# The product with w_out by Strassen's method, one product after the other for half the rows

## The chip, the cores and the metric

The kernel runs on one core of a Trainium2 chip. The core has five engines that run side by side and wait for each other through semaphores: TensorE (matrix products into PSUM), VectorE, ScalarE, GpSimd, and SyncE, which here only issues DMAs. DMAs are issued from three queues: SyncE's (SP), GpSimd's (POOL) and ScalarE's. The metric is the time of one execution on the device, in microseconds (us). Three runs of the kernel before gave 1147.69, 1149.69 and 1149.91 us; their median is 1149.69.

## The reference

One layer over 1024 rows of 1024 channels, all in float32. The input is normalized and modulated, multiplied by w_in (1024 x 8192), and goes through two branches: a dilated attention and a gated linear recurrence of eight heads (HGRN2). Their outputs are multiplied by w_branch_a and w_branch_b, weighted and added to y (1024 x 1024). The end is what matters here:

```python
y = sigmoid(g_a) * (o_a @ w_branch_a) + sigmoid(g_b) * (o_b @ w_branch_b)
x = x + gate[:, None] * (y @ w_out)        # gate: one factor for each of 1024 columns, from c and w_ada
return x * rsqrt(mean(x * x, -1) + EPS) * final_g
```

## The kernel before, in words

**Numbers as two parts.** A float32 operand of a large product is split into a high part (rounded to fp32r by a ScalarE copy) and a low part (the difference, by VectorE). A product is then three matmuls: high by high, low by high, high by low (`mm3`, lines 238 to 241). `split` (line 243) makes both parts of a 128 x 512 piece in the ring tiles w_hi and w_lo, four deep.

**Products with w_in.** They already use Strassen's method in Winograd's form: `add_pair` (line 265) takes two columns of 128 of w_in, four pieces of 256 KB, and makes seven products of 12 matmuls in place of eight. Its preparation steps (`prep_s1`, `prep_12` and so on) are the sums and splits of the pieces. The right-hand blocks, made once from the normalized input, are called b11, b12, b21, b22, t1 to t4.

**The stream.** `Stream` (line 71) keeps all these steps in one list. `step` runs a quarter of a product; `ahead` emits the preparation of the two steps that follow (`AHEAD`, line 67). Pieces are loaded by SP into a ring of eight raw tiles; a load goes out when its tile's last use has been emitted. `put_off` keeps a pair's seventh product back until two products of the next unit have been queued.

**Stages.** After a start of some 100 us, attention runs (to about 455 us), with stream steps filled in between its own matmuls. Then the attention branch (`branch_a`, line 1001) to about 541, with the pairs of heads 0 and 1 ahead of it. Then the recurrence, eight heads of some 51 us (`recurrence`, line 1072): in seven levels VectorE multiplies kk and qb by decays (lines 1117 and 1119), TensorE multiplies the results in small products (lines 1085, 1104, 1113), and pairs of w_in for the later heads are filled in (`fill`). From about 965 on comes the recurrence's branch (`branch_b`, line 1225): eight units of 128 rows of y, m0 to m7, whose results are split into parts as they come (lines 1237 to 1241). Meanwhile `gate_sum` (line 1316) computes the gate from w_ada's last third, loaded by SP, and `add_wo` (line 1283) loads w_out by SP, multiplies it by the gate and splits it.

**The last stage** (lines 1391 to 1413) multiplies y by the gated w_out. For rows 0 to 511 the eight PSUM banks hold four row tiles of 1024 columns, and the inner index k runs outermost; the tiles of rows 512 to 1023 follow one after the other. That is eight products of half the rows, half the columns and half of k. `finish` adds the residual x, squares, takes the root (GpSimd, `pow`), scales by final_g and stores each row tile; the last tile is cut in pieces of 512, 256 and 256 columns.

**Order.** TensorE's order is the program's throughout. That of the other engines is chosen by a scheduler when the kernel is built; each then runs its own list in that order.

## Time and profile before

| what | value |
|---|---|
| median of three runs | 1149.69 us |
| the profiled execution's own time | 1151.74 us |
| its span, first to last instruction | 1149.9 us |
| TensorE busy | 1113.1 us, 97% |
| VectorE busy | 809.0 us, 70% |
| ScalarE busy | 517.8 us, 45% |
| moved by DMA | 189.54 MB, mean 165 GB/s |
| mean granted TensorE clock | 0.995 |

The profile names engines PE (TensorE matmul), PEld (its weight loads), DVE (VectorE), ACT (ScalarE), POOL (GpSimd) and SP (SyncE). A row of a group or of a timeline gives line, engine, operation and the tiles written and read (`out<-in`); a bracket tells how long the engine was idle before it and what released it. Times are microseconds from the start of the span. The matmul of 512 columns is recorded with 0.39 us, but a new one starts every 0.23 us: matmuls overlap.

### The profile page before, as it was taken

Reading aid. Unit: us, or ns where it says so; the run is one execution under the profiler, and the core shown is the slowest. Engines: PE = TensorE matmul, PEld = TensorE weight load, DVE = VectorE, ACT = ScalarE, POOL = GpSimd, SP = SyncE. Lnnn points to the kernel's source line nnn. Section 1 sums busy time; section 2 is a strip of 40 time slices with the busy share of each in tenths; the row PEclk is TensorE's granted clock in tenths of the full one; section 3 lists DMA queues with packets and bytes.
Section 4 is the critical chain, followed back from the end, with each engine's and each line's share of the span. In section 5 each row is a group of like instructions: output and inputs, shape, how many; then the busy total and the mean of one; then the engine's idle time right before and its main releaser. Section 6 shows DMA issues by size and latency. Waiting matters only on the chain.

```text
span 1149.9 us, 21616 instructions
## 1 busy us (share of the span) xinstructions
PE 1113.1 (97%) x8266; PEld 908.7 (79%) x8266; DVE 809.0 (70%) x1607; ACT 517.8 (45%) x1059; POOL 117.7 (10%) x195
## 2 busy tenths in 40 slices
PE   5899999999999999999999999999999999999997
PEld 2677788888888888788877878787887878888886
DVE  3458888888877776753687787878888773769053
ACT  4565555578555555542234434343443432334021
POOL 1103032122202201100000000000000011000000
PEclk9999999999999999999999999999999999999999
DMA  9718576565556533746635253444435289864052
GB/s 311 225 37 248 175 209 179 152 165 145 139 139 154 153 100 104 269 158 215 223 103 171 78 185 100 160 140 137 158 101 176 81 259 325 290 213 133 29 183 75
DMA packets 161480, 189.54 MB, mean 165 GB/s; under 512 B 11312, under 2 KB 107696, under 8 KB 161376
## 3 DMA queue, kind: packets, MB, share of 16 engines
q1 hardware_dynamic: 140080, 153.95, 41.9%
q0 software_dynamic: 20896, 33.60, 11.7%
q8 instruction: 65, 1.06, 0.4%
q10 hardware_dynamic: 400, 0.61, 0.2%
q14 instruction: 39, 0.32, 0.1%
HBM read 129.36 MB, written 58.76 MB: 164 GB/s over the span
## 4 chain that ended last, share of the span: by engine, by line
PE 82%; DVE 7%; issue 6%; DMA 2%; ACT 2%; POOL 1%; ACTq 0%; POOLq 0%; DVEq 0%; SPq 0%
PE m L239 16%; PE m L241 15%; PE m L240 15%; PE pq L240 5%; PE pq L239 5%; PE pq L241 5%; PE pp L1085 3%; PE po L927 2%; PE pt L912 2%; PE pss L895 1%; PE pss L894 1%; PE pou L1168 1%; PE pou L1170 1%; PE pou L1153 1%; PE pmod L572 1%
## 5 line engine op out<-in xcount | busy, mean ns | idle before, releaser
L224 DVE TENSOR_TENSOR w_lo<-w_raw,w_hi 128x512 fp32r<-128x512 f32 x156 | 106.7, 686 | 49.6 <-ACT w_hi L246 45.8
L246 ACT CAST w_hi<-w_raw 128x512 fp32r<-128x512 f32 x146 | 90.4, 620 | 56.6 <-PE m L241 46.6
L327 ACT COPY ct<-m 128x512 f32<-128x512 f32 x90 | 52.6, 585 | 89.9 <-PE m L241 72.7
L246 ACT CAST w_hi<-w_s 128x512 fp32r<-128x512 f32 x90 | 55.8, 620 | 75.7 <-PE m L241 50.3
L274 DVE TENSOR_TENSOR ct<-m,ct 128x512 f32<-128x512 f32 x90 | 61.8, 687 | 27.7 <-PE m L241 26.1
L224 DVE TENSOR_TENSOR w_lo<-w_s,w_hi 128x512 fp32r<-128x512 f32 x90 | 61.9, 688 | 11.7 <-ACT w_hi L246 10.0
L900 ACT ACTIVATE s<-s,st 128x128 f32<-128x128 f32 (+3 forms) x64 | 49.8, 778 | 32.1 <-DVE st L897 32.1
L916 ACT CAST pth<-pt 128x512 fp32r<-128x512 f32 (+1 forms) x80 | 43.6, 544 | 36.3 <-PE pt L912 31.9
L224 DVE TENSOR_TENSOR ptl<-pt,pth 128x512 fp32r<-128x512 f32 (+1 forms) x80 | 50.5, 632 | 7.7 <-ACT pth L916 7.0
L239 PE MATMUL m<-b11h,w_hi 128*128 128x512 f32 x124 | 52.5, 424 | 2.0 <-DVE ct L274 2.0
L1176 POOL TENSOR_TENSOR ssh<-ssh,halfh 128x4 f32<-128x4 f32 x16 | 18.0, 1127 | 345.8 <-DVE ssh L1175 345.8
L239 PE MATMUL m<-b21h,w_hi 128*128 128x512 f32 x124 | 51.3, 414 | 0.6 <-ACT w_hi L246 0.6
L239 PE MATMUL m<-b22h,w_hi 128*128 128x512 f32 x124 | 50.9, 411 | 0.1
L239 PE MATMUL m<-t1h,w_hi 128*128 128x512 f32 x120 | 50.5, 421 | 0.0
L239 PE MATMUL m<-t2h,w_hi 128*128 128x512 f32 x120 | 49.6, 413 | 0.8 <-ACT ct L327 0.8
L239 PE MATMUL m<-t4h,w_hi 128*128 128x512 f32 x120 | 49.7, 414 | 0.4 <-DVE ct L274 0.4
L239 PE MATMUL m<-t3h,w_hi 128*128 128x512 f32 x120 | 49.7, 414 | 0.0
L241 PE MATMUL m<-b11l,w_hi 128*128 128x512 f32 x124 | 49.6, 400 | 0.0
L240 PE MATMUL m<-b11h,w_lo 128*128 128x512 f32 x124 | 49.2, 397 | 0.0
L240 PE MATMUL m<-b21h,w_lo 128*128 128x512 f32 x124 | 48.6, 392 | 0.2 <-DVE w_lo L224 0.2
L241 PE MATMUL m<-b21l,w_hi 128*128 128x512 f32 x124 | 48.8, 393 | 0.0
L241 PE MATMUL m<-b22l,w_hi 128*128 128x512 f32 x124 | 48.7, 393 | 0.0
(358 smaller groups left out, 3191.2 us busy)
## 6 DMA issues: line engine op xcount, KB each, us to landing
w_raw<-in_w_in_dram SPq DMA_DIRECT2D x128, 256.0 KB, 3.4
wa<-in_w_ada_dram SPq DMA_DIRECT2D x16, 512.0 KB, 8.7
qk_d<-ct SPq DMA_DIRECT2D x32, 256.0 KB, 3.4
k<-qk_d POOLq DMA_DIRECT2D x64, 128.0 KB, 4.9
qp<-qk_d POOLq DMA_DIRECT2D x32, 128.0 KB, 4.4
toep<-toep_d POOLq DMA_DIRECT2D x8, 512.0 KB, 6.2
vq_d<-ct SPq DMA_DIRECT2D x16, 256.0 KB, 2.6
vq<-vq_d POOLq DMA_DIRECT2D x16, 256.0 KB, 4.1
```

Source lines behind the costliest of these rows:

```text
L224: nc.vector.tensor_tensor(out_, a, hi.bitcast(F32), ALU.subtract)
L239: nc.tensor.matmul(ps, ah, bh, start=start, stop=False, skip_group_check=more)
L240: nc.tensor.matmul(ps, al, bh, start=False, stop=False, skip_group_check=more)
L241: nc.tensor.matmul(ps, ah, bl, start=False, stop=stop, skip_group_check=more)
L246: nc.scalar.copy(hi, src)
L274: nc.vector.tensor_tensor(out_, a, b_, op)
L327: nc.scalar.copy(c[name], b[which])
L900: nc.scalar.activation(s[:, :kw], s[:, :kw], AF.Exp, bias=prev, scale=-1.0, accum_out=st2[:, 2:3])
L912: nc.tensor.transpose(pt[:, c0:c0 + P], pn[b][:, kt * P:(kt + 1) * P], ident)
L916: nc.scalar.copy(pth[:, :w], pt[:, :w])
L927: nc.tensor.matmul(po[:, 256 - n:256], vq[kt // 4][:, kt % 4], src[:, c0:c0 + n], start=kt == 0 and a == 0, stop=kt == 2 * j + 1 and a == 1)
L1085: nc.tensor.matmul(pl[32 * b:32 * b + 32, c], kk[:, o:o + 32], qb[:, 2 - n:2, o:o + 32], start=True, stop=True)
```

## The change

**Strassen's method for y @ w_out.** w_out's seven right-hand blocks (512 x 512 each: b11, b21, b22 and four combinations t1 to t4) are no longer gated. They are loaded, combined and split ahead of time, in 16 groups (`wo_group`: kind 0 to 3, k 0 to 3), and stored as high and low part in DRAM (`wo_d`, 14 blocks of 1 MB; two combinations also unsplit in `wt_d`). A group loads two pieces through the stream's ring. Each of the first pairs takes one group (`more`), whose one or two parts are emitted after `prep_12` and `prep_s3`; the units of `branch_a` share four groups (`post`). So three groups go with the pairs of heads 0 and 1, four with `branch_a`, and nine with the first nine pairs of the recurrence.

**branch_b.** y stays unsplit (four blocks `Y[kh, th]`). VectorE's order is the program's from here to the end. The gate is summed from four loads of 1 MB on POOL's queue instead of eight of 512 KB on SP's.

**The last stage** runs seven products one after the other, each over four row tiles of one half of the rows: 48 matmuls each. The left-hand blocks are made from y on the way (`y_s1` to `y_s4`, `y_12`, `y_22`). The right-hand blocks are loaded by POOL (`load_wo`), two products ahead, into two pairs of buffers. Results are first summed with what was kept, then multiplied by the gate, then added to x. Rows end (root, scaling, store) in steps that `end_on` emits one result later. In the attention branch, the first `branch_a` unit also changes: with `amid` the put-off product of the pair before runs in the middle of it.

```diff
@@ add_pair @@
+        others = more()
+        def other():
+            if others:
+                others.pop(0)()
...
         def prep_12():
             parts = split(T(i12))
             stream.done(i12)
+            other()
...
@@ add_unit(..., post=None, amid=False) @@
+        if amid:
+            owed, stream.owed = stream.owed, None
...
-                return parts
+                if kh == n - 1 and post:
+                    post()
+                return parts, owed and owed[0]()
...
                     if th == 0:
                         yield
+                        if owed:
+                            yield from owed[1](put_off)
+                            yield
...
+    WO = ("b11", "b21", "t1", "t2", "b22", "t3", "t4")
+
+    def wo_group(kind, k):
+        def load(src):
+            def go(n):
+                raw = raw_tile(n)
+                nc.sync.dma_start(raw.rearrange("p a b -> p (a b)"), src)
+                return raw
+            return stream.piece(go)
+        rows = lambda kh, c: w_out[(4 * kh + k) * P:(4 * kh + k + 1) * P, 512 * c:512 * c + 512]
+        ids = [load(src) for src in ((rows(0, 0), rows(0, 1)), (rows(0, 1), rows(1, 1)),
+                                     (wt_d[0, k], rows(0, 0)), (wt_d[1, k], rows(1, 0)))[kind]]
...
+        def keep(name, n):
+            for p, part in enumerate(split(T(n))):
+                nc.sync.dma_start(wo_d[2 * WO.index(name) + p][:, k], flat(part).bitcast(F32))
+        def combine(name, a, b_, op, n=None):
+            nc.vector.tensor_tensor(T(0), T(a), T(b_), op)
+            if n is not None:
+                nc.sync.dma_start(wt_d[n, k], flat(T(0)))
+            keep(name, 0)
+            stream.done(*ids)
+        return [[lambda: keep("b11", 0), lambda: combine("t1", 1, 0, ALU.subtract)],
+                [lambda: keep("b22", 1), lambda: combine("t3", 1, 0, ALU.subtract, 0)],
+                [lambda: combine("t2", 0, 1, ALU.add, 1)],
+                [lambda: keep("b21", 1), lambda: combine("t4", 1, 0, ALU.subtract)]][kind]
...
     with ExitStack() as mg:
+        mg.enter_context(tc.manual_schedule(engines={mybir.EngineType.DVE}))
...
+                nc.vector.tensor_tensor(Y[m // 4, th][:, m % 4], ya[th], gb[th], ALU.add)
...
-                    nc.vector.tensor_tensor(raw, raw, gate[:, half_of(c)], ALU.mult)
...
+        def load_wo(i):
+            pool, name = ((hpool, "t4"), (m1, "mb"))[i % 2]
+            wos[i] = [block(pool, name + p, F32R) for p in "hl"]
+            for p in range(2):
+                nc.gpsimd.dma_start(wos[i][p].bitcast(F32), wo_d[2 * i + p])
+        def split_y(src, slot):
+            ...
+            for k in (0, 2):
+                nc.scalar.copy(hi[:, k:k + 2], src[:, k:k + 2])
+                sub(lo[:, k:k + 2], src[:, k:k + 2], hi[:, k:k + 2])
...
+            def result(name, t0, c):
+                def f(n, ps):
+                    u, sl = kept[name][:, n], slice(512 * c, 512 * c + 512)
+                    if t0 + n == 7:
+                        xr, s4 = row(7)
+                        r = gated(ps[:, 256:], slice(256, 512))
+                        nc.vector.tensor_tensor(xr[:, 256:512], r, xr[:, 256:512], ALU.add)
+                    nc.vector.tensor_tensor(u, ps, u, ALU.add)
+                    nc.vector.tensor_tensor(u, u, gate[:, sl], ALU.mult)
+                    add_in(t0 + n, sl, u, c)
+                    end_on()
+                    if t0 == 0 and c == 1:
+                        end(t0 + n)
+                return f
+            def last(n, ps):
+                sl = slice(0, 512)
+                add_in(4 + n, sl, gated(ps, sl), 0)
+                end_on()
+                end(4 + n)
+            def last_part(a, ps):
+                ...
+                if a == 0:
+                    nc.vector.tensor_tensor(xo[:, 512:], xr[:, 512:], fg[:, 512:], ALU.mult)
+                add_in(7, sl, gated(ps, sl), 2 * a)
+                nc.vector.tensor_tensor(xo[:, sl], xr[:, sl], fg[:, sl], ALU.mult)
+                if a == 0:
+                    end_on()
+                    ...
+                    end_on()
...
+            prep = {0: [(1, y_12, None), (2, y_s1, (hpool, "b11"))], 2: [(3, y_s2, (hpool, "t1")), (4, y_s4, (m1, "ma"))],
+                    3: [(5, y_s3, (hpool, "b11")), (6, y_22, None)]}
+            plan = [(A, True, keep("p1")), ("B", True, result("p1", 0, 0)), ("C", True, keep("p5")),
+                    (A, False, keep("u2")), ("C", False, result("u2", 0, 1)), (A, False, result("p5", 4, 1)),
+                    (A, False, last)]
+            load_rows(range(4))
+            for i, (banks_, start, then) in enumerate(plan):
+                for j, y, slot in prep.get(i, ()):
+                    ys[j] = y(slot)
+                if i == 4:
+                    load_rows(range(4, 8))
+                ...
+                if i + 2 < 7:
+                    load_wo(i + 2)
```

`gated` multiplies a PSUM result by the gate; `add_in` adds it to the residual row and squares it on ScalarE; `end(t)` queues the two ending steps of a row tile (root on VectorE and GpSimd; scaling and store), of which `end_on` emits one per call for every tile under way. `combine` and `y_s1` to `y_s4` add or subtract blocks of y in two VectorE operations of 1024 columns each; `y_12` and `y_22` only split.

315 lines of the change are left out of this document (187 added, 128 removed).

## The prediction

> **What bounds the kernel now.** I read the page first (busy time, the chain that ended last), then the busy time by stage, then the instructions of the stage that changes and of the stages that receive its preparation.
>
> ```profile
> span 1149.9 us, 21616 instructions
> PE 1113.1 (97%) x8266; PEld 908.7 (79%) x8266; DVE 809.0 (70%) x1607; ACT 517.8 (45%) x1059; POOL 117.7 (10%) x195
> PE 82%; DVE 7%; issue 6%; DMA 2%; ACT 2%; POOL 1%; ACTq 0%; POOLq 0%; DVEq 0%; SPq 0%
> ```
>
> TensorE sets the time: 97% busy, 82% of the chain. A change gains what it takes from TensorE's queue and loses whatever makes TensorE wait. Busy time by stage (TensorE, its weight loads, VectorE, ScalarE, GpSimd, granted clock, DMA share, GB/s) and the ends of the product with w_out:
>
> ```profile
> 455.00:541.00 86.00, 83.53 (x359) 67.25 (x358) 48.87 (x77) 36.62 (x65) 6.64 (x13) 0.98 0.68 216
> 541.00:965.00 424.00, 418.51 (x4789) 340.27 (x4788) 331.64 (x634) 166.99 (x388) 26.60 (x32) 1.00 0.48 156
> 965.00:1054.90 89.90, 89.90 (x394) 73.78 (x394) 60.12 (x92) 31.85 (x56) 1.22 (x3) 1.00 0.72 235
> 1054.90:1143.20 88.30, 88.30 (x409) 73.26 (x408) 32.33 (x57) 15.71 (x40) 3.88 (x7) 1.00 0.29 99
> L239 PE MATMUL pq<-w_hi,t3h x34: 280/389/397, 1054.9 to 1140.7; 128*128 128x512 f32 x30, 128*128 128x256 f32 x4
> 1143.08 0.28 PE L241 MATMUL pq<-t2l,yh 128*128 128x256 f32 x1
> ```
>
> The last stage, 1054.9 to 1143.2, is TensorE alone: 88.3 us without a gap, while VectorE works 32.3 us of it. The group shown is one of twelve of equal size, so the stage is 12 x (30 + 4/2) = 384 matmuls of 512 columns, 88.3 / 384 = 0.230 us each. In the recurrence, 541 to 965, VectorE is 78% busy beside TensorE's 99%.
>
> **Part 1, seven products for eight.** Seven products of 48 matmuls take 336 x 0.230 = 77.3 us: **11.0 us less** on TensorE. The start stays at 1054.9 plus what earlier stages lose: the first product needs only the first four rows of y and block b11.
>
> **Part 2, VectorE in the last stage.** Gate and sums move to the results. Twelve results (products two, five and six) cost three operations each (sum, gate, residual), four of the last product two; before, 17 additions did. Prices:
>
> ```profile
> 1036.72 4.29 DVE L1296 TENSOR_TENSOR w_raw<-w_raw,gate 128x512 f32<-128x512 f32 x7
> 1030.41 0.68 DVE L1237 TENSOR_TENSOR gbr<-pq,gbr 128x512 f32<-128x512 f32 x1
> 1031.13 0.69 DVE L1238 TENSOR_TENSOR yar<-yar,gbr 128x512 f32<-128x512 f32 x1
> 1111.52 1.28 DVE L1367 SCALAR_TENSOR_TENSOR xo<-xr,s,fg 128x1024 f32<-128x1024 f32 x1 [0.76 <-POOL s L1366]
> 1112.72 1.28 DVE L1355 TENSOR_TENSOR xr<-pq,xr 128x512 f32<-128x512 f32 x2
> 1133.69 0.16 DVE L1364 TENSOR_TENSOR s<-s 128x1 f32<-128x1 f32 x1 [0.85 <-ACT jko L1357]
> 1133.89 0.15 DVE L1365 TENSOR_SCALAR s<-s 128x1 f32<-128x1 f32 x1
> 1134.79 1.28 DVE L1367 SCALAR_TENSOR_TENSOR xo<-xr,s,fg 128x1024 f32<-128x1024 f32 x1 [0.75 <-POOL s L1366]
> 1140.53 0.42 DVE L1355 TENSOR_TENSOR xr<-pq,xr 128x256 f32<-128x256 f32 x1 [1.44 <-PE pq L241]
> 1140.99 0.42 DVE L1372 TENSOR_TENSOR xo<-xr,fg 128x256 f32<-128x256 f32 x1
> ```
>
> Back to back, an operation of 512 columns comes every (4.29 - 0.68) / 6 = 0.60 us; one that needs the result before it every 0.72; a scaling of 1024 columns takes 1.20; 256 columns in a dependent row 0.46; a small one 0.20; a row's root through GpSimd returns 0.90 after the second small one. A result is thus 0.72 + 0.72 + 0.60 = 2.04 us, and four to a product of 11.04 us fit. But from the fifth product on VectorE also ends rows. From there it owes eight results 16.3, the extra half of the last tile 0.9, seven scalings 8.4, seven root pairs 2.8, six operations of the last product 4.0, the first half of the last tile with its small sums 2.4: **34.8 us**, in a written order, so nothing passes a wait. It starts with the fifth product's first result, 4 x 11.04 + 2.76 + 0.2 = 47.1 us after the stage began, idles 1.4 while results are still rarer than its work, and waits 0.6 for the last row's root, because two scalings stand between the two halves of the last tile. It reaches the last 256 columns at 47.1 + 34.8 + 1.4 + 0.6 = 83.9, TensorE ended at 77.3. So the end comes 6.4 us later behind TensorE (83.9 less the 77.5 at which the columns are there), and 0.46 for one more dependent operation. Before, the tail held only this:
>
> ```profile
> 1143.40 0.42 DVE L1355 TENSOR_TENSOR xr<-pq,xr 128x256 f32<-128x256 f32 x1 [1.46 <-PE pq L241]
> 1144.76 0.55 POOL L1378 TENSOR_TENSOR s<-s,halff 128x1 f32<-128x1 f32 x1 [10.00 <-DVE s L1377]
> 1145.34 0.72 ACT L1379 ACTIVATE xo<-xo,s 128x512 f32<-128x512 f32 x1 [0.92 <-POOL s L1378]
> 1146.09 0.38 ACTq L1380 DMA_DIRECT2D out_dram<-xo  x1
> ```
>
> Last stage: -11.0 + 6.4 + 0.46 = **-4.1 us**. Bounds: -10.5 if VectorE were never late (the 0.46 stays), -2.7 if all 34.8 us went at the dependent pace, 4% more. The preparation of y (8 subtractions of 512 columns and 16 operations of 1024: 8 x 0.60 + 16 x 1.20 = 24 us of VectorE) and the second product's results, 8.2, lie within the 47.1 us before and cost nothing; without that cover they would lengthen the same backlog.
>
> **Part 3, w_out's halves from DRAM.** Two loads of 1 MB per product, issued on GpSimd when the product two before ends: 2.1 MB in 11.0 us.
>
> ```profile
> b21h<-ob_d POOLq DMA_DIRECT2D x2, 512.0 KB, 7.8
> 940.00:950.00 10.00, 10.00 (x60) 8.15 (x61) 4.63 (x8) 5.04 (x10) 2.11 (x4) 1.00 1.00 332
> xr<-in_x_dram SPq DMA_DIRECT2D x8, 512.0 KB, 4.0
> ```
>
> At 332 GB/s 2.1 MB take 6.3 us, and 512 KB landed in 4.0 to 7.8, of which 1.6 is transfer: 2.4 of latency, 8.7 in all. That fits, except for the fifth product's blocks: x rows 4 to 7 (2.1 MB) go out while they load, and 4.2 MB take 12.7 + 2.4 less the head start of about 3. I take **0.5 us**, bounds 0 (x first lands) and 4 (all 15.1 against 11.0). GpSimd's queue behind a waiting load holds only later loads and the roots of finished rows. By the Trainium skill's page "DMA: Bandwidth & Descriptors" (Anatomy of one DMA), a transfer of this queue costs 2.0 us plus bytes over 436 GB/s, an estimate of 6.8 us for 2.1 MB; by that the term would be 0, and no load of 1 MB is in this trace.
>
> **Part 4, preparation moved ahead.** 16 groups make 28 splits (a ScalarE cast, a VectorE subtraction) and 16 combinations: 44 VectorE and 28 ScalarE operations, 32 loads and 64 stores on SP. Removed are the splits of w_out and of y in the stages after 965, hidden there. Seven groups fall on 455 to 541, where VectorE is 57% busy: nothing, at most their 21 x 0.60 = 12.6. Nine (23 VectorE operations, 14 casts) fall on the first five of the eight heads of the recurrence. There VectorE changes kk and qb just before TensorE multiplies them:
>
> ```profile
> 572.19 0.69 DVE L1119 TENSOR_TENSOR qb<-qb,tot 128x512 f32<-128x512 f32 x1
> 573.62 0.58 PE L1085 MATMUL pp<-qb,kk 128*32 128x32 f32 x43
> 624.34 0.68 DVE L1119 TENSOR_TENSOR qb<-qb,tot 128x512 f32<-128x512 f32 x1
> 625.08 0.41 PE L1085 MATMUL pp<-qb,kk 128*32 128x32 f32 x26 [0.51 <-DVE qb L1119]
> 793.48 0.69 DVE L1119 TENSOR_TENSOR qb<-qb,totn 128x512 f32<-128x512 f32 x1
> 794.80 0.56 PE L1113 MATMUL pp<-qb,kk 128*64 128x64 f32 x6
> 680.00:690.00 10.00, 10.00 (x193) 7.70 (x193) 9.99 (x22) 3.57 (x6) 0.00 (x0) 1.00 0.41 133
> ```
>
> Of the 30 such pairs of these heads the first and the last are shown, with slacks of 0.74 and 0.63 us, and the tightest, 0.06, where TensorE did wait. An operation of 0.60 ahead of a pair exceeds its slack by 0.15 on average over the 30. These levels fill about half of a head, so half of 23 operations meet them: 11.5 x 0.15 = **1.7 us**. Bounds: 0 (they go where VectorE idles) and 23 x 0.60 = 13.8 (every one on the path). A group also takes slots of the four-deep ring of split tiles, so one product of each pair is prepared one product ahead instead of two. The six pieces a pair now loads share a ring of eight, so loads are issued about a pair's length later, and on SP, behind a load that waits for its slot, stand the result stores; six result tiles cover that. Both are priced within these bounds.
>
> **Part 5, the gate vector by GpSimd loads.** 4 MB and two bias rows leave SP for GpSimd, behind ob's loads. Nothing waits on them before 1031, and the first w_out blocks behind them have till 1054.9, 24 us for 4.2 MB or 12.7 by the rate above: nothing, 0 to 4.
>
> **Sum.** -4.1 + 0.5 + 1.7 = -1.9 on the profiled execution, whose span is 1149.9 (its own time 1151.7, 2.0 above the median shown; I carry the difference over): 1149.7 - 1.9 = **1147.8 us**.
>
> **Rivals.** *Slower: the recurrence pays in full.* VectorE is full in the levels (9.99 of 10 us above), and once slack is used up each inserted operation moves TensorE by 0.60. With all 23 on the path, -4.1 + 0.5 + 13.8 = +10; with the 11.5 in the levels, 6.9, it is +3.3, or 1153.0. It decides from 3.6 + 2.3 = 5.9 us of waits on. For it: the tight pairs. Against: the levels' other work (subtractions for products two steps ahead) can give way.
>
> *The wait at 483 goes or grows.* ScalarE stood behind a late load and TensorE idled 2.0 us, then ran at half pace:
>
> ```profile
> 482.82 0.39 PE L241 MATMUL m<-t3l,w_hi 128*128 128x512 f32 x1
> 485.22 0.47 PE L239 MATMUL m<-b11h,w_hi 128*128 128x512 f32 x1 [2.01 <-DVE ct L274]
> 487.18 0.63 PE L240 MATMUL m<-b11h,w_lo 128*128 128x512 f32 x1
> 487.60 0.63 PE L241 MATMUL m<-b11l,w_hi 128*128 128x512 f32 x1
> 480.00:490.00 10.00, 7.99 (x29) 6.12 (x28) 6.81 (x13) 7.30 (x14) 0.00 (x0) 0.83 0.69 242
> ```
>
> A pitch of 0.42 for 0.23 at a mean clock of 0.83 over 10 us costs 1.7 more, 3.7 in all. The change reorders the first branch product and loads just there; without the wait, 1147.8 - 3.7 = 1144.1. Against: it adds loads to the same queue. The Trainium skill's page "TensorE: Matmul & The Clock Gate" (HAM oscillation) warns only of idle gaps above some 3.4 us; by that a wait of 2 us costs itself and 1.7 less. The trace disagrees here: 2.01 us sufficed.
>
> *VectorE is not the bound at the end.* Then part 2 costs 0.46 alone: 1149.7 - 10.5 + 0.5 + 1.7 = 1141.4. For: 30 us of TensorE remain from the fifth product's first result. Against: 34.8 of work in a written order.
>
> *It doesn't do what it says*: eight products' worth of matmuls would show at once; the plan has seven entries, so I give it nothing.
>
> **How the numbers follow.** Differences under 0.2% (2.3 us) can't be told from none here. Chances: forecast 0.45, slower rival 0.23, the wait at 483 gone 0.17, VectorE not the bound 0.13, 0.02 for worse. The forecast's own range is 1145.6 (nothing lost in parts 3 and 4) to 1151 (3 us more lost there); it stands on the edge, so 0.19 of its 0.45 are faster and 0.24 the same, 0.02 slower. Faster: 0.19 + 0.17 + 0.13 = 0.49; same: 0.24 + 0.03 of the slower rival's mild end = 0.27; slower 0.24. The range runs from VectorE nearly unbound, 1140.5, past the slower rival's 1153.0 to 1154.5.
>
> **What would show it.** Right: seven products of 11.0 us without gaps; last matmul to last VectorE reading of PSUM some 6 us instead of 0.3; scalings of two rows between the last tile's halves; TensorE's waits on qb and kk in the recurrence up by 1 to 3 us. Wrong: TensorE waiting for the loaded blocks, a tail under 5 us behind the last matmul, or waits in the recurrence above 6.

## The result, and the profile after

The changed kernel takes **1178.68 us** (median of four runs, 1176.32 to 1180.03) against 1148.83 for the kernel before on the same chip: a ratio of **1.0258**, 95% interval 1.0237 to 1.0279. It is 2.6% slower; the forecast was 1147.8.

The page of the changed kernel: its span, busy time, and the shares of the chain that ended last.

```profile
span 1177.2 us, 21768 instructions
...
PE 1112.7 (95%) x8206; PEld 904.8 (77%) x8206; DVE 851.3 (72%) x1668; ACT 535.8 (46%) x1085; POOL 130.2 (11%) x215
...
PE 77%; DVE 8%; DMA 7%; ACT 3%; issue 3%; POOL 1%; SPq 0%; POOLq 0%; DVEq 0%; ACTq 0%
```

TensorE has one product of eight less to do and is busy for as long as before (1112.7 against 1113.1). Its idle time grew from 1149.9 - 1113.1 = 36.8 us to 1177.2 - 1112.7 = 64.5, and matmuls ran slower in the stages ahead of the last one. DMA's share of the chain went from 2% to 7%.

The same by stage. First the kernel before, cut at its own boundaries: just behind attention (455 in both), the recurrence's first and last product of qb and kk on line 1085 (1159 in the kernel after), the first product with w_out, and the end of that stage in the kernel after. The kernel before has its last stage in the prediction's rows, 88.3 us. Then the kernel after, cut at the same events. Columns: TensorE, weight loads, VectorE, ScalarE, GpSimd, granted clock, DMA share, GB/s.

```profile
455.00:569.60 114.60, 112.13 (x482) 90.36 (x480) 65.25 (x101) 44.67 (x79) 7.70 (x15) 0.99 0.66 212
569.60:936.10 366.50, 362.36 (x4474) 294.13 (x4475) 298.50 (x575) 146.85 (x342) 17.07 (x17) 1.00 0.43 138
936.10:1054.90 118.80, 117.45 (x608) 96.81 (x596) 76.88 (x127) 43.93 (x89) 9.68 (x17) 1.00 0.80 258
```

```profile
455.00:579.60 124.60, 115.44 (x484) 91.63 (x486) 74.96 (x119) 51.60 (x92) 7.21 (x14) 0.96 0.88 284
579.60:966.30 386.70, 368.58 (x4475) 298.20 (x4477) 312.99 (x602) 154.87 (x357) 17.45 (x17) 0.98 0.53 167
966.30:1085.10 118.80, 117.46 (x606) 96.79 (x593) 61.39 (x102) 34.05 (x70) 15.80 (x26) 1.00 0.77 261
1085.10:1163.30 78.20, 78.20 (x349) 63.73 (x347) 61.28 (x87) 28.37 (x55) 8.21 (x16) 1.00 0.59 222
```

The seven products take 78.2 us against 88.3. The stage ahead of them takes 118.8 in both. All of the loss lies where the blocks of w_out are prepared: 10.0 us in the stretch from attention to the recurrence and 20.2 in the recurrence. The product with w_out starts 30.2 us late. Of these 30.2 us, 20.7 are idle TensorE (27.3 us idle in the two stretches for 6.6 before), and 9.5 are matmuls that took longer (484.0 us busy for 474.5) at a lower granted clock, 0.96 and 0.98. The first stretch has DMA at 0.88 instead of 0.66.

Who waited there, 455 to 966 of the kernel after. Columns: us in total, times, longest.

```profile
ACT w_hi L248 <- DMA wo_d<-w_hi: 33.8, 16, 3.4
DVE w_lo L226 <- DMA wo_d<-w_lo: 13.9, 9, 8.1
PE pp L1159 <- DVE qb L1193: 11.5, 5, 4.8
...
PE m L241 <- DVE ct L281: 4.6, 2, 3.2
ACT w_hi L248 <- DMA wo_d<-w_lo: 4.0, 1, 4.0
```

ScalarE's casts and VectorE's subtractions wait for **stores**. A split tile from which a part is being stored to DRAM (`wo_d`) can't be written again until the store has landed, and the groups' splits use the ring of four that TensorE's next products are split into. The chain of waits shows how that reaches TensorE at 588 (start, duration, what):

```profile
579.56 4.98 DMA wo_d<-w_hi
...
584.63 0.63 ACT w_hi L248
...
585.30 0.69 DVE w_lo L226
586.00 0.46 DVE ct L473
586.45 0.33 DVE dg L1171
586.79 0.07 DVE kk L1191
...
587.73 0.59 DVE qb L1193
...
588.37 1.08 PE pp L1159 x64
```

The cast waits for a store that lands after 5 us. VectorE executes in order, so its subtraction waits for the cast, and behind it stand kk and qb, which have nothing to do with w_out but which TensorE multiplies next. TensorE waited 4.76 us here, as its timeline shows:

```profile
588.37 1.08 PE L1159 MATMUL pp<-qb,kk 128*32 128x32 f32 x64 [4.76 <-DVE qb L1193]
```

### The profile page after: what moved, and what is told of

Same layout as the page of the kernel before. It is cut to its first block, busy times and chain, and to the rows that moved or that the text cites. A ratio compares the mean times of both kernels' runs of the same rounds, so it can differ in the third digit from the quotient of the medians.

```text
span 1177.2 us, 21768 instructions
## 1 busy us (share of the span) xinstructions
PE 1112.7 (95%) x8206; PEld 904.8 (77%) x8206; DVE 851.3 (72%) x1668; ACT 535.8 (46%) x1085; POOL 130.2 (11%) x215
## 4 chain that ended last, share of the span: by engine, by line
PE 77%; DVE 8%; DMA 7%; ACT 3%; issue 3%; POOL 1%; SPq 0%; POOLq 0%; DVEq 0%; ACTq 0%
PE m L241 15%; PE m L243 14%; PE m L242 14%; PE po L988 3%; PE pt L973 3%; PE pq L242 2%; PE pq L243 2%; PE pq L241 2%; DMA wo_d<-w_hi 2%; PE pp L1159 2%; DMA wo_d<-w_lo 2%; DVE w_lo L226 2%; PE pss L956 2%; PE pss L955 1%; PE fa L242 1%
## 5 line engine op out<-in xcount | busy, mean ns | idle before, releaser
L226 DVE TENSOR_TENSOR w_lo<-w_raw,w_hi 128x512 fp32r<-128x512 f32 x180 | 122.8, 687 | 78.7 <-ACT w_hi L248 60.5
L248 ACT CAST w_hi<-w_raw 128x512 fp32r<-128x512 f32 x174 | 106.9, 619 | 98.7 <-PE m L243 48.6
L281 DVE TENSOR_TENSOR ct<-m,ct 128x512 f32<-128x512 f32 x90 | 61.7, 686 | 21.7 <-PE m L243 20.2
L226 DVE TENSOR_TENSOR w_lo<-w_s,w_hi 128x512 fp32r<-128x512 f32 x90 | 61.7, 686 | 14.6 <-ACT w_hi L248 12.3
L243 PE MATMUL m<-b11l,w_hi 128*128 128x512 f32 x124 | 50.2, 405 | 0.0
L1159 PEld LDWEIGHTS pp<-qb,kk 128*32 128x32 f32 x2560 | 29.2, 112 | 26.7 <-issue 16.4
```

Source lines behind the costliest of these rows:

```text
L226: nc.vector.tensor_tensor(out_, a, hi.bitcast(F32), ALU.subtract)
L243: nc.tensor.matmul(ps, ah, bl, start=False, stop=stop, skip_group_check=more)
L248: nc.scalar.copy(hi, src)
L281: nc.vector.tensor_tensor(out_, a, b_, op)
L1159: nc.tensor.matmul(pl[32 * b:32 * b + 32, c], kk[:, o:o + 32], qb[:, 2 - n:2, o:o + 32], start=True, stop=True)
```

## The experiments

Let H be the theory that **held split tiles** cost the time: tiles of the ring of four that can't be written again until a store from them has landed. It has three rivals: V, the 44 inserted VectorE operations (my slower rival); L, the groups' loads, which share the raw ring and SyncE's queue; D, the DMA traffic of the stores. A later rival, Q, is that stores standing in SyncE's queue block the loads behind them.

All runs, as ratios to the kernel before in the same session, with 95% intervals, and three durations from each profile: from attention's last product with v (452.4 before, 451.9 after) to the first product of qb and kk in the recurrence (the line named above), from there to the last one of that line, and the start of the product with w_out. From that last one to this start every kernel takes 118.8 or 118.9.

| Run | us | ratio (interval) | to the recurrence | recurrence | w_out starts |
|---|---|---|---|---|---|
| before | 1148.83 | 1 | 117.2 | 366.5 | 1054.9 |
| changed | 1178.68 | 1.0258 (1.0237-1.0279) | 127.7 | 386.7 | 1085.1 |
| no preparation | 1143.28 | 0.9950 (0.9933-0.9966) | 112.8 | 366.6 | 1050.1 |
| no stores | 1145.91 | 0.9980 (0.9969-0.9992) | 114.4 | 370.1 | 1053.4 |
| stores of a constant block | 1157.48 | 1.0070 (1.0047-1.0092) | 115.2 | 370.0 | 1066.0 |
| no loads | 1157.68 | 1.0078 (1.0055-1.0100) | 120.2 | 374.2 | 1066.1 |
| stores by GpSimd | 1186.51 | 1.0342 (1.0315-1.0368) | 135.3 | 390.2 | 1094.5 |
| stores by ScalarE | 1191.15 | 1.0366 (1.0344-1.0389) | 139.6 | 387.8 | 1097.5 |
| result ring of 4, no stores | 1156.95 | 1.0068 (1.0049-1.0087) | 112.3 | 371.2 | 1065.2 |
| result ring of 4, own pair | 1181.53 | 1.0290 (1.0264-1.0316) | 128.8 | 380.2 | 1091.2 |
| small stores | 1152.96 | 1.0035 (1.0019-1.0051) | 119.0 | 371.5 | 1060.0 |
| small stores, raw source | 1151.02 | 1.0014 (1.0003-1.0025) | 115.8 | 373.2 | 1060.2 |
| raw source | 1161.64 | 1.0104 (1.0087-1.0121) | 122.8 | 374.5 | 1067.2 |
| later groups | 1168.21 | 1.0162 (1.0139-1.0185) | 121.1 | 382.4 | 1073.6 |
| parts in place | 1167.17 | 1.0166 (1.0133-1.0199) | 128.8 | 371.5 | 1071.8 |
| later and in place | 1171.46 | 1.0199 (1.0173-1.0224) | 127.0 | 381.8 | 1077.6 |
| placed | 1173.73 | 1.0218 (1.0198-1.0238) | 113.0 | 379.5 | 1081.5 |
| placed, in place | 1166.20 | 1.0159 (1.0141-1.0177) | 113.4 | 377.3 | 1070.8 |
| tail by GpSimd | 1177.23 | 1.0262 (1.0244-1.0281) | 127.8 | 381.1 | 1077.0 |

The durations are from one execution each. The last row runs the changed kernel's code up to the product with w_out, and its recurrence took 381.1 instead of 386.7, so a difference of some 6 us in one of these columns is not to be read; the verdicts go by the ratios.

### What the preparation costs, and which part of it

The whole preparation left out, and in a second run its stores alone. In both the last stage reads pieces of w_out in place of the stored parts (and the groups that read a stored sum back load another piece of w_out instead):

```diff
-        return wo_group(*groups.pop(0)) if groups else []
+        return []
...
-                nc.gpsimd.dma_start(wos[i][p].bitcast(F32), wo_d[2 * i + p])
+                nc.gpsimd.dma_start(wos[i][p], kp(w_out)[:, 4 * p:4 * p + 4, 512 * (i % 2):512 * (i % 2) + 512].bitcast(F32R))
```

> The changed kernel without the preparation of w_out: no group is loaded, combined, split or stored, and the last stage loads pieces of w_out itself as its right-hand blocks, so the product with w_out is left out of what is computed (traffic of the last stage unchanged in size). It prices the last stage, the gate sum and the new order alone. In the changed kernel the last stage begins at 1085.1 us in place of 1054.9 and lasts 92.1 us to the end of the span in place of 95.0. All theories of the preparation say the same here if it alone is the cause of the 30.2 us: span about 1149.9 - 2.9 = 1147, ratio 0.9975. If the new order of the first branch unit or the gate's loads cost something, it is above 1150.

```diff
-            for p, part in enumerate(split(T(n))):
-                nc.sync.dma_start(wo_d[2 * WO.index(name) + p][:, k], flat(part).bitcast(F32))
+            split(T(n))
...
-            if n is not None:
-                nc.sync.dma_start(wt_d[n, k], flat(T(0)))
```

> All loads, combinations and splits of the 16 groups as in the changed kernel, but none of the 64 stores to DRAM; the last stage loads pieces of w_out itself, so the product with w_out is left out of what is computed. Theory H (the split tiles of the groups stand in the ring of four that the products use, and are held until their stores have landed; ScalarE and VectorE wait for them in order, and TensorE behind these): the 30.2 us go down to 5 or less, time 1146 to 1152. Theory V (the 44 added VectorE operations in a VectorE that is full): 1173 to 1179, nothing changes. Theory L (the groups' loads share the ring of eight raw tiles, so the products' pieces come late): 1173 to 1179. Theory D (DMA traffic: 16.8 MB of stores slow every other transfer): in between, 1155 to 1165.

Without preparation 0.9950, with all of it but the stores 0.9980. The 44 VectorE operations, 28 casts and 32 loads together cost 0.30% or some 3 us; **V and L fall** as causes by themselves. The 64 stores cost the rest: 1.0258 - 0.9980 = 2.78%, some 32 us. TensorE's waits in the run without stores, 455 to 935:

```profile
PE pp L1154 <- DVE qb L1188: 2.4, 3, 1.1
...
PE pp L1173 <- DVE qb L1188: 0.8, 1, 0.8
```

The waits on qb are 3.2 us; with the stores those of L1159 alone are 11.5. Without stores the change is a gain of 0.2%.

### Stores that hold nothing, and no loads beside them

The 56 stores of parts read a block that has lain in SBUF from the start; in the other run the groups take their operands from that block and load nothing (their sums go into a tile of the split ring).

```diff
-                nc.sync.dma_start(wo_d[2 * WO.index(name) + p][:, k], flat(part).bitcast(F32))
+                nc.sync.dma_start(wo_d[2 * WO.index(name) + p][:, k], X["b11"][p][:, k].bitcast(F32))
```

> As the changed kernel, with the 56 stores of split parts in place, of the same size and in the same queue, but they read a block that does not change in this stage (b11) instead of the parts just split, so no split tile is held by a store; the product with w_out is thereby left out of what is computed. Theory H: near the kernel without stores, 1146 to 1153. Theories V and L: 1173 to 1179. Theory D: 1173 to 1179, since the traffic is the same. It tells H from D.

> As the changed kernel, but the groups load nothing: they combine and split the block b11 in place of pieces of w_out, with the same number of ScalarE and VectorE operations, ring tiles and stores; the product with w_out is thereby left out of what is computed. Theory L: 1146 to 1153, since the ring of raw tiles holds four pieces per pair again. Theories H and V: 1170 to 1179. Theory D: some us less than the changed kernel, 8.4 MB of 33.6 MB gone, 1170.

```diff
-        ids = [load(src) for src in ((rows(0, 0), rows(0, 1)), (rows(0, 1), rows(1, 1)),
-                                     (wt_d[0, k], rows(0, 0)), (wt_d[1, k], rows(1, 0)))[kind]]
-        T = lambda n: stream.tiles[ids[n]]
+        T = lambda n: X["b11"][n][:, k].bitcast(F32).rearrange("p (a b) -> p a b", a=4)
...
```

With the constant block no time is lost from attention to the end of the recurrence (115.2 and 370.0, as without stores). But the run isn't the clean test that it was meant to be: the stores had nothing to wait for and were all issued at 47 to 132 us, among the loads of the start:

```profile
L421 SPq DMA_DIRECT2D wo_d<-b11h x28: 319/480/1337, 47.6 to 126.5; - x28
```

There they cost some 10 us by themselves (1.0070 - 0.9980 = 0.90%): TensorE's busy time from 100 to 150 us fell from 46.2 in the changed kernel to 37.3, at a DMA share of 0.91 for 0.69. So the run shows that stores which hold nothing are not free where DMA is that busy, and doesn't separate H from D. Without loads the loss is about 1.0078 - 0.9980 = 0.98%, a third of what it was, though every store and every held tile is still there; no expectation had that (1157.7 lies between the ranges). H alone doesn't explain it. Loads and stores share DMA and SyncE's queue, and the loads also take raw tiles; this run doesn't tell which of these counts. It does show that the sum of the waits on stores is no measure of the loss: ScalarE and VectorE waited 50.2 us for them here and 51.7 in the changed kernel, but TensorE waited 7.8 us on qb for 14.0 (lines 1159 and 1178 of the changed kernel).

### Is it SyncE's queue, or the ring?

> The 64 stores of the preparation (56 of split parts, 8 of sums) are issued by GpSimd in place of SyncE; the split tiles are held as before. Theory of the held ring: the waits of w_hi and w_lo on the stores stay at 40 to 60 us and the time at 1172 to 1182, or above it where GpSimd's own waits (61 us at most for one head's sums) delay a store and hold a tile for as long. Theory of the queue: the loads of pieces are no longer behind the stores, the wait of w_s and the sums on loads (5 us) goes, and the time falls to 1148 to 1160.

> The same 64 stores are issued by ScalarE, which makes the cast and so reaches the store of the high part as soon as its data is there; the store of the low part has it wait for VectorE's subtraction. Theory of the held ring: the tiles are held for the landing alone (median 4.5 us) without the time that a store waits in SyncE's queue, so part of the loss goes, 1160 to 1174. Theory of the queue: SyncE's loads run free, 1146 to 1156, plus up to 28 x 0.7 = 20 us of ScalarE time for the waits on the subtractions, of which little is on the path. A third outcome, above 1178: ScalarE's own waiting for the low parts costs more than the queue did.

```diff
-                nc.sync.dma_start(wo_d[2 * WO.index(name) + p][:, k], flat(part).bitcast(F32))
+                nc.gpsimd.dma_start(wo_d[2 * WO.index(name) + p][:, k], flat(part).bitcast(F32))
...
-                nc.sync.dma_start(wt_d[n, k], flat(T(0)))
+                nc.gpsimd.dma_start(wt_d[n, k], flat(T(0)))
```

(and `nc.scalar` in the other run). Both got **slower**, 1.0342 and 1.0366, an outcome that both expectations allowed for an issuer with waits of its own: GpSimd waits up to 44.1 us at a time for one head's sums, and ScalarE must wait for the subtraction before it can store a low part. So these two runs alone don't refute Q. What speaks against it is its size: VectorE's waits for loaded pieces, through which a blocked load would act, are 6.2 us in all in the changed kernel (455 to 966), and fell only to 2.6 and 3.7 with SyncE's loads free of the stores. The small stores below stand in SyncE's queue just as these do, and cost 0.55% in all: **Q falls as the main cause**. ScalarE and VectorE still waited for the landings, 47.3 and 43.4 us with ScalarE as the issuer.

A pair of split tiles for the groups alone, whose 4 KB are taken from the result ring (four tiles for six), and its control, the same cut without stores:

```diff
-CT = 6
+CT = 4
...
-        hi = wpool.tile([P, 4, P], F32R, name="w_hi")
-        lo = wpool.tile([P, 4, P], F32R, name="w_lo")
+        pool, n = (own, "g") if own else (wpool, "w")
+        hi = pool.tile([P, 4, P], F32R, name=n + "_hi")
+        lo = pool.tile([P, 4, P], F32R, name=n + "_lo")
...
+    stream.own = gctx.enter_context(tc.tile_pool(name="gown", bufs=1, reuse_waits="tile"))
```

> The groups' parts get a pair of tiles of their own (one w_hi and one w_lo, from the end of attention to the end of the recurrence), so that no store holds a tile of the ring of four that TensorE's next products are split into; the 4 KB come from the result ring, cut from six tiles to four, whose own cost the run with the same cut and no stores gives. Loads, operations, stores and the issuing queue are those of the changed kernel. Theory of the held ring (split tiles are kept until their stores have landed and ScalarE and VectorE wait behind them in order): the waits of w_hi and w_lo on the stores (38 + 14 us in the changed kernel) shrink to the groups' own parts, and the time falls from 1178.7 to within 6 us of the run with the cut and no stores, some 1150 to 1156. Theory of the queue (the stores wait in SyncE's queue for their casts, 23 + 12 us, and later loads of pieces stand behind them): nothing of that is changed, so the time stays above 1168.

> Control for the run with the own pair: the result ring cut from six tiles to four, loads, combinations and splits of the blocks kept, no store of a part, the last stage reads pieces of w_out in their place (its output is not the reference's). The run without stores and with six tiles took 1145.9. If the cut costs nothing: 1144 to 1148; if the evictions wait for result tiles, up to 1152. Both theories expect the same here.

Inconclusive for H, and a miss. The control lost 11 us against the run with six tiles and no stores, all before attention's end (462.9 against 450.1), so the two are compared in the stretches. The pair opens when attention ends, and only half of the blocks came to lie in it:

```profile
wo_d<-w_hi SPq DMA_DIRECT2D x14, 256.0 KB, 4.5
...
wo_d<-g_hi SPq DMA_DIRECT2D x14, 256.0 KB, 3.3
```

Those of the stretch before the recurrence stayed in the ring, and it kept its loss (128.8 against 112.3). In the recurrence, where the pair served, 9.0 us are lost (380.2 against 371.2) instead of 16.6, a difference hardly above the 6 us named under the table. More split tiles with the result ring left whole weren't tried.

### Bytes and held tiles, two by two

Two edits that can be combined: each of the 56 stores of parts writes 64 of its 512 columns, so that an eighth of their bytes moves (the eight stores of sums stay whole, and the last stage reads pieces of w_out); and the stores read the unsplit raw tile, so that no split tile is held (a raw tile of the ring of eight is, for which SyncE's queue waits rather than ScalarE or VectorE).

```diff
-                nc.sync.dma_start(wo_d[2 * WO.index(name) + p][:, k], flat(part).bitcast(F32))
+                nc.sync.dma_start(wo_d[2 * WO.index(name) + p][:, k, 0:64], flat(part).bitcast(F32)[:, 0:64])
```

> Each of the 56 stores of split parts writes 64 of its 512 columns, an eighth of the bytes, and the last stage reads pieces of w_out in place of the parts (its output is not the reference's); the number of stores, the tiles they hold and the queue are those of the changed kernel. Theory of traffic (14.7 MB of stores slow the landings of everything else): the loss goes, 1146 to 1152. Theory of the held ring: the tiles are still held to the landing, which small stores reach in some 2.3 us (the least seen) against 4.5, so half of the waits of 52 us and half of the 33 us stay: 1157 to 1168.

```diff
-            for p, part in enumerate(split(T(n))):
-                nc.sync.dma_start(wo_d[2 * WO.index(name) + p][:, k], flat(part).bitcast(F32))
+            split(T(n))
+            for p in range(2):
+                nc.sync.dma_start(wo_d[2 * WO.index(name) + p][:, k], flat(T(n)))
...
```

> The stores read the unsplit raw tile in place of its two parts (twice the same 256 KB; the parts are still made, and the output is not the reference's): bytes, number and queue of the stores are those of the changed kernel, and no tile of the split ring is held by a store; held instead are tiles of the raw ring of eight, for which SyncE's queue waits and not ScalarE or VectorE. Theory of the held split ring: the waits of w_hi and w_lo on stores go and the time falls to 1147 to 1158. Theory of traffic: 1168 to 1180, as before. If a held raw tile costs as much as a held split tile: 1165 to 1185 too, then with VectorE's sums waiting for loads (w_s, more than 10 us).

> Small stores (64 of 512 columns) read from the raw tile: neither the bytes of the stores nor a split tile held; the number of stores, the queue, the loads and the operations are the changed kernel's (the output is not the reference's, and the last stage reads pieces of w_out). It is the fourth corner of bytes and held split tiles. If these two causes are all of it: 1145 to 1149, as without any store (1145.9). If the number of stores in SyncE's queue costs something by itself: 1150 to 1154, as with small stores of the parts (1153.0).

| ratio | raw tile held | split tile held |
|---|---|---|
| 32 KB a store | 1.0014 | 1.0035 |
| 256 KB a store | 1.0104 | 1.0258 |

Against 0.9980 without stores. The stores as such, small and holding no split tile, cost 0.34%, some 4 us. The bytes cost 0.90%, some 10 us. Holding split tiles costs 0.21% where the stores are small, hardly more than the intervals, and 1.54%, **some 18 us, where they carry 256 KB**. The large term is neither cause alone but both together. So the first two runs fell between the ranges that the single causes gave, and the third came as its second outcome, that the number of stores costs something by itself. A reading that fits is that a tile is held for as long as its store takes, and that large stores take longer. The waits on the stores and their time from issue to landing (min, median, max; transfers of wo_d from 400 to 900 us), in the changed kernel and then with small stores:

```profile
  ACT w_hi L248: 37.8, 17
  DVE w_lo L226: 13.9, 9
...
DMA to landing us min/median/max: 2.3/4.0/8.4
```

```profile
  ACT w_hi L248: 16.3, 15
  DVE w_lo L226: 9.0, 5
...
DMA to landing us min/median/max: 1.5/2.8/7.6
```

Nearly as many waits (20 for 26), half as long in all (25.3 us for 51.7). The 4.5 us that two expectations took for these stores is a median over all transfers of wo_d, the 1 MB loads of the last stage among them; the stores alone have 4.0. By the Trainium skill's page "DMA: Bandwidth & Descriptors" (Anatomy of one DMA, which is about GpSimd's queue: 2.0 us plus the bytes at 436 GB/s) a store of 256 KB takes an estimate of 2.6 us; the run with the stores on that queue has 2.6 as the least, but 4.1 as the median.

The columns differ in one thing more: a store of the raw tile needn't wait for the split, and these go out earlier, from 421 to 787 us for 453 to 815 with full stores. What of the 1.54% that is worth wasn't measured.

What the bytes cost without a held split tile is seen in what waits for loads, in the run with full stores from the raw tile, and in the one with small ones from it:

```profile
DVE w_raw L426 <- DMA w_raw<-in_w_out_dram: 12.4, 4, 6.0
DVE w_s L281 <- DMA w_raw<-in_w_in_dram: 10.2, 5, 5.5
```

```profile
DVE w_raw L426 <- DMA w_raw<-in_w_out_dram: 7.5, 4, 3.8
DVE w_s L281 <- DMA w_raw<-in_w_in_dram: 2.0, 3, 1.2
```

VectorE's waits for pieces are 22.6 us against 9.5. Whether those loads are late because of the traffic or because held raw tiles let them start late, these two runs don't tell apart.

### Can the loss be avoided by place, or in place?

The first moves three of the four groups of the branch a stage, where DMA is fullest, into the recurrence; the second moves all groups out of the stretch between attention and recurrence; the third writes each low part over its raw tile and most high parts into raw tiles, so that 12 of 56 stores hold a split tile.

```diff
-            todo = shared.setdefault(m // 2, None) or next_group()
+            todo = shared.setdefault(m // 2, None) or (next_group() if m // 2 >= 3 else [])
```

> Three of the four groups that the changed kernel prepares in the branch a stage (six of its sixteen pairs of stores before 600 us) are moved into the recurrence, one group to a pair of columns; nothing else differs. Theory of the held ring with slow landings: in the branch a stage DMA is at 0.85 to 0.88 and stores land late, in the recurrence at 0.5; with fewer groups in the busy stretch the loss before the recurrence falls from 15 us (579.6 against 564.5 without stores) to about 8, that in the recurrence (387 us against 370) grows by less, to 390, and the time is 1170 to 1177. If each held tile costs the same wherever it lies, 1176 to 1182. If DMA traffic in the busy stretch is all of it, the first loss goes and the second stays: 1163 to 1168.

```diff
...
-    pair_iz(0)
+    pair_iz(0, next_group)
...
-    pair_fq(0, next_group)
+    pair_fq(0)
...
```

> The sixteen groups are put where DMA is least busy: five with pairs of columns in the second half of attention (gates a and b and the first head of i and z; DMA at 0.3 to 0.6 there), none from the end of attention to the recurrence (DMA 0.85 to 0.88 in the changed kernel), eleven in the recurrence (0.45). Splits, ring and stores as in the changed kernel. Theory that the loss is held tiles times late landings: the 15 us lost before the recurrence shrink to 0 to 4; the recurrence keeps a loss of about the 12 us that the run with later groups had there (382 against 370): 1156 to 1165. If every held tile costs the same wherever it lies (33 us for 56 stores): 1174 to 1182. If attention pays more than the stretch after it did, because TensorE has no idle time there: above 1170.

```diff
-            for p, part in enumerate(split(T(n))):
+            j = {"t2": 1, "b11": 2, "b22": 2, "b21": 2}.get(name)
+            hi = wpool.tile([P, 4, P], F32R, name="w_hi") if j is None else T(j).bitcast(F32R)
+            nc.scalar.copy(hi, T(n))
+            sub(T(n).bitcast(F32R), T(n), hi)
+            for p, part in enumerate((hi, T(n))):
...
```

> The low part is written over the raw tile itself, and the high part of the blocks b11, b21, b22 and of t2 into a raw tile (for the first three a tile of the raw ring of eight that nothing is loaded into); only the high parts of t1, t3 and t4 take a tile of the split ring: 12 of 56 stores hold one. The kernel computes what the changed one does. Theory of the held split ring: 1152 to 1163, and if the raw ring (then with up to seven of eight tiles in use by a group and its pair of columns) is short of tiles, up to 1170 with waits on loads. Theory of traffic: 1172 to 1185.

> The same placement, with the low parts written over the raw tiles and most high parts in raw tiles (12 of 56 stores hold a tile of the split ring). The run with parts in place passed the recurrence in 371.5 us, against 370.1 without stores; it lost 17 us before it, in the stretch that has no groups now. Theory of held tiles times late landings: 1147 to 1154, at or near the kernel before (1149). If raw tiles are short in attention as well: 1155 to 1165.

> Parts in place (12 of 56 stores hold a split tile) and three of the four groups of the branch a stage moved into the recurrence; the kernel computes the result. The two edits alone gave 1167.2 and 1168.2 against 1178.7. If they act on different shares of the loss: 1155 to 1162. If both remove the same share, or the tiles of the raw ring now set the pace: 1163 to 1169. Below 1149, the kernel before, neither theory puts it.

Each edit returns some of the loss (1.0162, 1.0166 and, hardly beyond the intervals, 1.0218 for 1.0258), two of them together return no more than one, within the intervals (1.0159 and 1.0199), and **none of these reaches the kernel before**. Both pairs came out above every range given for them; the later groups, 1168.2, lie between the range of H and the edge of that of D; the parts in place came within the range for a raw ring short of tiles. Place isn't the answer: the groups put into attention left the next stretch clean (113.0) and cost attention 18 us, at a DMA share of 0.62, lower than that of the stretch they had left:

```profile
300.00:400.00 100.00, 91.31 (x465) 75.55 (x464) 70.13 (x168) 50.68 (x106) 16.87 (x30) 0.95 0.62 169
```

TensorE was busy for all of the 100 us there in the changed kernel, and for 91.3 here. My expectation that half-empty DMA makes held tiles cheap was wrong; the outcome named third there is the one that came. In place, ScalarE's and VectorE's waits on the stores fell from 51.7 us to 14.9 (7.3 when placed too), but waits for loads took their place, 13.1 us for w_s and 12.3 for the sums of w_out against 5.1 and 1.1:

```profile
ACT w_hi L248 <- DMA wo_d<-w_hi: 14.9, 5, 7.7
DVE w_s L281 <- DMA w_raw<-in_w_in_dram: 13.1, 10, 8.4
...
DVE w_raw L429 <- DMA w_raw<-in_w_out_dram: 12.3, 4, 5.2
```

A tile must be held somewhere until its store has landed, and both rings feed TensorE. Why the later groups and the parts in place together (1.0199) gain nothing over either alone stays open; their intervals overlap. What the trace shows is that VectorE's waits for pieces of w_in are then 22.3 us, for 13.1 in place and 6.2 with the later groups.

### VectorE at the end

```diff
                 def scale():
-                    nc.vector.scalar_tensor_tensor(xr, xr, s4[:, 3:4], fg, ALU.mult, ALU.mult)
+                    if t in (5, 6):
+                        nc.scalar.mul(xr, xr, s4[:, 3:4])
+                    else:
+                        nc.vector.scalar_tensor_tensor(xr, xr, s4[:, 3:4], fg, ALU.mult, ALU.mult)
                     nc.sync.dma_start(out[P * t:P * t + P, :], xr)
+                if t in (5, 6):
+                    nc.gpsimd.tensor_tensor(xr, xr, fg, ALU.mult)
```

> In the changed kernel, the rows of tiles 5 and 6 are multiplied by the final gain on GpSimd, as soon as they are summed, and by their root on ScalarE, in place of one VectorE instruction of 1.28 us each, which stand between the halves of the last tile. If VectorE sets the end of the last stage (it reached the last 256 columns 5.3 us after TensorE's last product): 2.6 us less VectorE work on the path, 1175 to 1177 against 1178.7. If GpSimd takes over 6 us for a product of 128x1024 or slows VectorE beside it, nothing or a loss: 1178 to 1183.

Two scalings of VectorE at the end go to GpSimd and ScalarE. 1177.23 us, 1.0262: no gain. VectorE has two scalings of 1.28 us less and still reaches the last 256 columns later: 1162.16, 7.1 us after TensorE's last matmul starts (1155.03), where the changed kernel has 5.5 (1168.60 after 1163.12). The last stage from its start to the end of the span is 1170.7 - 1077.0 = 93.7 against 92.1. Its timelines of GpSimd and of VectorE:

```profile
1152.74 2.40 POOL L1512 TENSOR_TENSOR b21h<-b21h,fg 128x1024 f32<-128x1024 f32 x1
1156.58 2.50 POOL L1512 TENSOR_TENSOR b21l<-b21l,fg 128x1024 f32<-128x1024 f32 x1 [1.44 <-ACT jko L1487]
```

```profile
1153.20 2.48 DVE L1485 TENSOR_TENSOR b21l<-w_s,b21l 128x512 f32<-128x512 f32 x1
...
1156.81 2.29 DVE L1501 TENSOR_TENSOR s<-s 128x1 f32<-128x1 f32 x1
```

An addition that takes 0.69 us elsewhere took 2.48, and a single column 2.29 instead of 0.15: neither ended before GpSimd's product had, at 1155.1 and 1159.1. That is the slowing that the expectation had as its second outcome. What was taken from VectorE came back as waiting.

## Why the prediction was wrong, step by step

The last stage in the kernel after: TensorE's last matmul, VectorE at the last 256 columns, the issue of ScalarE's last store.

```profile
1163.12 0.28 PE L243 MATMUL fc<-t4l,w_hi 128*128 128x256 f32 x1
```

```profile
1165.20 1.28 DVE L1506 SCALAR_TENSOR_TENSOR b21h<-b21h,s,fg 128x1024 f32<-128x1024 f32 x1
...
1167.40 1.28 DVE L1506 SCALAR_TENSOR_TENSOR b21l<-b21l,s,fg 128x1024 f32<-128x1024 f32 x1 [0.41 <-POOL s L1503]
1168.60 0.42 DVE L1491 TENSOR_TENSOR w_s<-fc,gate 128x256 f32<-128x256 f32 x1
```

```profile
1171.69 0.37 ACTq L1565 DMA_DIRECT2D out_dram<-t2l  x1
```

**Part 1** held: 78.2 us for 77.3, no gaps. **Part 2** held in its mechanism: VectorE reaches the last columns 5.3 us behind TensorE (1168.6 less the stage's end at 1163.3; forecast 6.4), with two scalings between the last tile's halves. Another 1.7 us, which it didn't have, went after the last operation (5.5 us from ScalarE's store to the end of the span, 3.8 before). From the start of the product to the end of the span it is 95.0 before and 92.1 after: -2.9 for the forecast's -4.1 + 0.5 = -3.6. **Part 3** was 0.5 too high: no matmul of the last stage waited for a block. Here are the median landings of the loads of four of the seven blocks, high and low part of 1 MB each, issued together:

```profile
t4h<-wo_d POOLq DMA_DIRECT2D x4, 1024.0 KB, 5.1
t4l<-wo_d POOLq DMA_DIRECT2D x4, 1024.0 KB, 8.3
```

The second lands after 8.3 us, against the 8.7 that the prediction worked out from rows. The Trainium skill's page "DMA: Bandwidth & Descriptors" (Anatomy of one DMA) gave an estimate of 6.8. **Part 5** held: the 118.8 us of the stage after the recurrence are unchanged. So the gate by GpSimd's loads cost nothing, and the splits of w_out that were removed there had indeed been hidden.

**Part 4 is the step that failed**: +1.7 with 13.8 as the upper bound, and +30.2 measured. It priced the inserted operations, and that size was about right (loads, splits and sums without stores: some 3 us). It listed the 64 stores on SP and gave them no price. It saw that a group takes slots of the ring of four and reduced that to "one product of each pair is prepared one product ahead instead of two", and then wrote that "both are priced within these bounds", which were bounds of VectorE's time. What the sentence lacks is *how long* a slot is taken. A slot of a product comes free when TensorE is done with it. A slot of a stored part comes free when the store has landed, and ScalarE and VectorE wait for that in order, with kk and qb behind them. The rows at hand allowed an estimate: 56 stores, each holding a tile for about 4 us (the quoted landings, of loads of 512 KB, were 4.0 to 7.8), make 56 x 4 = 224 us of holding in a ring of four pairs. No row of the trace excluded that this reached TensorE, so 13.8 was no upper bound. The runs put in its place: some 3 us for the operations and loads, some 32 for the stores, and of these some 18 only where a store both holds a split tile and carries 256 KB. Of the measured 30.2, 9.5 are slower matmuls, which no term of the prediction's sum had. The prediction's own mark for "wrong" (waits in the recurrence above 6) did show it: 11.5 us on qb alone.

**The rivals.** The slower one had the sign and not the mechanism: VectorE's inserted operations are not what cost the time, and its 1153.0 is 26 us short. *The wait at 483 goes* came true where nothing is stored: that wait of 2.0 us is in neither trace, without preparation or without stores, and from attention to the recurrence takes 112.8 and 114.4, against 117.2 before. That is 2.8 to 4.4 us for the 3.7 priced, though differences of this size are within what one execution varies. In the changed kernel longer waits stand there. *VectorE is not the bound at the end* is out: it was 5.3 us late.

**The sum.** -2.9 in the last stage and +30.2 before it make +27.3, which is the difference of the profiled spans, 1177.2 - 1149.9. The gain of the last stage is real and survives in the run without preparation (0.9950); ten times as much was lost ahead of it.

## What to carry to other kernels

When work is moved ahead and its results are stored, the store's source tile belongs to the store until it has landed: ask whose ring the tile comes from, how many landings (by the loaded trace, not the idle one) fit between two uses of a slot, and what stands in order behind the instruction that waits. A pass that only adds time on idle engines can cost a multiple of that by shortening a ring which feeds the engine that sets the time. Try such a change first without its stores: that run separated the 3 us of the operations from the 32 of the stores, which no count of instructions did.

## What the runs showed of the hardware that was not expected

A wait of TensorE of two or three us can cost more than itself, because matmuls run slower after it. The kernel after, its TensorE timeline at 466 us and its row of the 10 us around it:

```profile
462.84 0.39 PE L243 MATMUL m<-t3l,w_hi 128*128 128x512 f32 x1
466.46 0.77 PE L241 MATMUL m<-b11h,w_hi 128*128 128x512 f32 x1 [3.23 <-DVE ct L281]
...
467.98 0.63 PE L241 MATMUL m<-b11h,w_hi 128*128 128x512 f32 x1
468.41 0.63 PE L242 MATMUL m<-b11h,w_lo 128*128 128x512 f32 x1
```

```profile
460.00:470.00 10.00, 6.77 (x23) 5.10 (x22) 4.88 (x9) 2.90 (x5) 0.54 (x1) 0.77 0.74 261
```

After 3.23 us without a matmul the pitch is 0.43 us instead of 0.23 for some five us, and the granted clock of the 10 us is 0.77. Such stretches fit the 9.5 us of added busy time ahead of the last stage: TensorE was as busy as before with an eighth of its last product gone. The Trainium skill's page "TensorE: Matmul & The Clock Gate" (HAM oscillation) puts the gap that does this above some 3.4 us; here 3.23 and, before the change, 2.01 sufficed.

GpSimd's products of 128x1024 took 2.40 and 2.50 us, and VectorE's instruction beside each ended only after it. The Trainium skill's page "SBUF — State Buffer" (Terms, shared port pair) says of these two engines that the loser "fully blocks"; the trace agrees, with 2.48 us for an addition of 0.69.

Two tiles fewer in the result ring, whose tiles are also held by stores until they land, cost 0.88% (1.0068 against 0.9980), all of it before attention's end (462.9 against 450.1): in attention that ring has no slack to give.
